# Margins on the steps of chains, an event for the rebuild of x, and later modulation sums in a two-layer diffusion trunk

## The chip, the cores and the metric

The kernel runs on 1 core of one Trainium2 chip. The metric is the device time of one execution in microseconds (us), as the median over repeated runs. The core has the matrix engine TensorE (PE in the rows, its weight loads PEld), VectorE (DVE), ScalarE (ACT), GpSimd (POOL), and SyncE (SP), which starts the DMA transfers here. Each engine works through its own instructions in the order of the program and waits for the others by semaphores.

## The reference

One inference step of a trunk with two layers for 640 tokens (128 context tokens and 512 latent ones) of width 1024. Each layer has a mixer and an MLP:

```python
def _block(x, mod, mixer, g, b, w1, w2):
    sh1, sc1, gt1, sh2, sc2, gt2 = jnp.split(mod, 6, axis=-1)
    mix, aux = mixer(x * (1 + sc1) + sh1)
    x = _layer_norm(ALPHA * x + gt1 * mix, g[0], b[0])
    hf = x * (1 + sc2) + sh2
    ff = jnp.square(jax.nn.relu(hf @ w1)) @ w2
    x = _layer_norm(ALPHA * x + gt2 * ff, g[1], b[1])
    return x, aux
...
mod_ctx = jnp.einsum('d,lde->le', jax.nn.silu(c_ctx), w_mod) + b_mod
mod_lat = jnp.einsum('bd,lde->lbe', jax.nn.silu(c), w_mod) + b_mod[:, None, :]
```

The mixer of layer 0 (even) is retention beside differential attention, that of layer 1 (odd) windowed attention beside gated linear attention (GLA). Both have one input projection and one output projection. The MLP goes from 1024 to 4096 and back. The modulation vector `mod` of a layer has 6 x 1024 values for each of two conditions (context, latent), and costs a pass over a 1024 x 6144 weight.

## The kernel before, in words

The 640 tokens are 5 tiles of 128. Every large matmul is made of three products of fp32r halves: a weight is split into `whi` (a cast on ACT) and `wlo` (a subtraction on DVE), an activation likewise (`hh`/`hl`, `cath`/`catl`, `ghi`/`glo`), and PE sums hi x hi, hi x lo and lo x hi. A step of 24 matmuls (8 chunks of the contraction by 3 products) is the unit in which the program is written.

The program is laid out by a planner in Python, the class `Order`. It keeps a model clock `now` and a queue of modelled operations for each engine. `product` moves `now` on with each matmul, so the written order of PE is the program order. For the other engines the order is that in which the model starts the operations, and it is pinned with dependencies (`follow`). On the chip each engine then keeps to that order whatever the true times are; the model has no say in when something runs.

Small work is written as generators, the *chains*: `spawn` starts one, a chain yields between its steps, and `ready` decides when its next step may be written. A bare `yield` means that all operations issued by the step before must have ended in the model; a number means a delay in model time; a callable means an event. `gemm` writes one large matmul step: first every chain that is ready, then `background()` (splits and loads of weights, and a step of the modulation every few us of model time), then the matmuls. So a chain's transposes and small matmuls stand in PE's order between the large steps, and the large steps that stand between a chain's last vector operation and the matmul that reads it are its *cover*.

Names that the prediction uses:

- **Modulation.** A chunk of 512 columns is made of 8 pieces of `w_mod`, loaded by DMA into `wmod` (3 buffers, `MRAW`). POOL multiplies a piece by the conditioning column and adds it into its accumulator `moda` (a TENSOR_SCALAR and a TENSOR_TENSOR), DVE does the other condition into a `moda` of its own, whose first piece ACT writes. `ModChunk.finish` then has PE sum over the partitions (`modps`, ones x `moda`), and DVE adds the bias (`brow`). In layer 0 this goes on through the mixer and the MLP, for the chunks that come later.
- **norm** (L859): the layer norm of a token tile after the output projection (key "m") and after the MLP (key "h"). It normalises `x` on POOL, transposes it (`lnT`), applies modulation into `hh`/`hl` for the matmuls that come next, and starts `update()`: x = x * g + b, in place, four TENSOR_TENSOR of 128x512 on POOL for a tile, `x<-x,lnrow` in the rows, 20 for the five tiles. The sum that reads this x comes only at the end of the next mixer or MLP.
- **Even mixer.** Per head: `qkT` transposes, `sd` scores, softmax `p`, `wT` transposes, `odp` products, normed `od`, `catT` transposes into `cath`/`catl`. `U` are the state products of retention.
- **Odd mixer.** At its end: `po` (GLA's output in PSUM), copies to `o` on ACT, head norm (`hbn`, `hmv`, `hve`, `rsq`, `nmr` on DVE, then `o<-o,nmr,rsq` on ACT), the gate `o<-o,sg` on POOL, `catT` transposes, `cath` (ACT) and `catl` (DVE), then the output projection `ops`. The output projection is made in two halves of the contraction, env 0 and env 1: 240 matmuls of the first half (5 tiles x 2 column halves x 24) can run before GLA is done; the second half reads `catT` of `o`.
- **MLP.** Eight groups of 512 hidden units, g0 to g7. A group is `ff` (192 matmuls, ~28 us), relu squared (`relu`, `ghi`, `glo`), then `fps` (five token tiles t, 24 matmuls each) and `y` sums.

Of the kernel before, what the change touches and what calls it, by code (L numbers as in the profile page):

```python
# [35 lines left out]
DEC0, DEC = 0.0, 2.0  # L36
MOD_SPACE = (4.0, 3.6)
LO_POOL = 0
UPD = (40.0, 30.0)
DRS = False  # L40
WD = 3
WS = 2
MRAW = 3
NSMALL = 4


C_ID = 0
# [80 lines left out]
class Order:  # L128
# [181 lines left out]
        self.chains.append(c)  # L310

    def ready(self, c):
        if c[2] > self.now or not all(self.over(x) for x in c[1]):
            return False
        if c[3] == "s":
            return any(self.vacant(x) for x in self.rings.get("s", [None]))
        return c[3] is None or c[3]()
# [87 lines left out]
def trunk_kernel(ctx: ExitStack, tc: tile.TileContext, io: dict, layers: int = 2, stop: str = ""):  # L405
# [21 lines left out]
    def slot(s):  # L427
        t = gpool.tile([P, SLOT], F32, tag="g", name=nm(s))
        order.ring_of[t.tensor.name] = "g"
        return t  # L430
# [118 lines left out]
    class ModChunk:  # L549
# [36 lines left out]
        def finish(self):  # L586

            l, a = self.l, self.c % 2
            kind = self.c // 2
            if a == 0:  # L590
                mods[l, kind] = dram.tile([2, 2, 512], F32, name=nm("mrow"))
            ps = acc("modps")
            b = self.b
            for j in range(4):
                mm(ps[32 * j:32 * j + 32, :256], ones[:, 0:32], self.A[j % 2][:, 256 * (j // 2):256 * (j // 2) + 256],
                   start=True, stop=True)
            dve.tensor_tensor(b[:, :256], ps[:, :256], b[:, :256], op=ALU.add)
            for r in range(2):
                load(mods[l, kind][r, a, :].rearrange("(e n) -> e n", e=2), b[32 * r:32 * r + 65:64, :256])
            if kind not in (2, 5):  # L600
                if a == 0:
                    cols[l, kind] = const.tile([P, 8, 2], F32, name=nm("mcol"))
                for r in range(2):
                    load(cols[l, kind][:, 4 * a:4 * a + 4, r], mods[l, kind][r, a, :].rearrange("(b p) -> p b", p=P))
            done.add(("mod", l, self.c))
            yield 0.0

    done = set()
# [247 lines left out]
            pool.tensor_tensor(y, y, rows[1 if t == 0 else 0][a][:, :512], op=ALU.mult)  # L856
            stt(x, x, ALPHA, y, op0=ALU.mult, op1=ALU.add)

    def norm(t, rows, ft, A, B, final, key, xd=None):  # L859

        cuts = [(0, 0, 512), (1, 0, 512)] if t < NT - 1 else [(0, 0, 256), (0, 256, 512), (1, 0, 256), (1, 256, 512)]
        st = sm("bn", [P, 4, 6])[:, :len(cuts), :]
        mv = sm("mv", [P, 2])
        for i, (a, c0, c1) in enumerate(cuts):
            dve.bn_stats(st[:, i, :], X[t][a][:, c0:c1])
        dve.bn_aggr(mv, st)
        if DRS:
            ve = sm("ve", [P, 1])
            dve.tensor_scalar(ve, mv[:, 1:2], EPS, None, op0=ALU.add)
            r = rsqrt(ve, [P, 1])  # L870
        else:
            ve = sm("ve", [P, 1])
            sq = sm("sq", [P, 1])
            act.activation(sq, mv[:, 1:2], AF.Sqrt, bias=eps_t)
            dve.tensor_scalar(ve, mv[:, 1:2], EPS, None, op0=ALU.add)
            r = sm("r", [P, 1])
            q = sm("q", [P, 1])
            dve.reciprocal(r, sq)
            vec_tt(q, r, r, op=ALU.mult)
            stt(q, q, -0.5, ve, op0=ALU.mult, op1=ALU.mult)  # L880
            stt(r, q, 1.5, r, op0=ALU.add, op1=ALU.mult)
        nmr = sm("nmr", [P, 1])
        stt(nmr, mv[:, 0:1], -1.0, r, op0=ALU.mult, op1=ALU.mult)
        if not final:
            xn = X[t]
            for a in range(2):
                pool.tensor_scalar(xn[a][:, :512], xn[a][:, :512], r, nmr, op0=ALU.mult, op1=ALU.add)
        time = order.step[:]
        if final:

            cut = (1024, 1024, 1024, 512, 256)[t]
            for a, c0, c1 in ((0, 0, 256), (0, 256, 512), (1, 0, 512)) if t == NT - 1 else ((0, 0, 512), (1, 0, 512)):
                c, far = slice(c0, c1), 512 * a + c1 <= cut
                x, g, b = X[t][a][:, c], rows[0][a][:, c], rows[1][a][:, c]
                if far:
                    act.activation(x, x, AF.Identity, scale=r, bias=nmr)
                    pool.tensor_tensor(x, x, g, op=ALU.mult)
                    pool.tensor_tensor(x, x, b, op=ALU.add)
                else:
                    stt(x, x, mv[:, 0:1], g, op0=ALU.subtract, op1=ALU.mult)  # L900
                    stt(x, x, r, b, op0=ALU.mult, op1=ALU.add)
                load(io["y"][t * P:(t + 1) * P, 512 * a + c.start:512 * a + c.stop], x)
            return
        def update():
            for a in range(2):
                x = xn[a][:, :512]
                pool.tensor_tensor(x, x, rows[0][a][:, :512], op=ALU.mult)
                pool.tensor_tensor(x, x, rows[1][a][:, :512], op=ALU.add)
                yield 3.0
            if xd is not None:  # L910
                for a in range(2):
                    load(xd[a], xn[a][:, :512])
            done.add(("x", *key))
        yield time
        yield "s"
        tp = pss("lnT")
        for k in range(KT):
            transpose(tp[:, tcol(k)], xn[k // 4][:, tcol(k % 4)])
        r_ = 1 if t == 0 else 0
        for a in range(2):  # L920
            h = slot("h32")
            for b in range(4):
                k = 4 * a + b
                act.activation(h[:, tcol(b)], tp[:, tcol(k)], AF.Identity,
                                     scale=A[:, k, r_:r_ + 1], bias=B[:, k, r_:r_ + 1])
            h4 = h[:, :512].rearrange("p (b c) -> p b c", b=4)
            hi = ft.h[a][:, :, tcol(t)]
            act.copy(hi, h4)
            (pool if a < LO_POOL and t < NT - 1 else dve).tensor_tensor(ft.l[a][:, :, tcol(t)], h4, hi.bitcast(F32), op=ALU.subtract)
        order.spawn(update(), UPD[xd is not None])  # L930
        yield
        done.add(key)

# [3 lines left out]
    ft = FT("h0")  # L937
# [542 lines left out]
    def odd_mixer(ft, cat, out_half):  # L1480
# [208 lines left out]
        def sq(m):  # L1689
            st = W[m]  # L1690
            st["q"] = [slot("sqT"), slot("sqT")]

            def post(t, ps):
                qq = slot("qq")
                if t == 0:
                    act.copy(qq[:, :256], ps[:, :256])
                else:
                    a = rope(ps[:, :256], t, 4)
                    vec_tt(qq[:, :256], a[:, :256], a[:, 256:512], op=ALU.add)

                def turn():
                    tp = acc("sqT")
                    for b in range(2):
                        transpose(tp[:, tcol(b)], qq[:, tcol(b)])
                    for b in range(2):
                        act.copy(st["q"][b][:, tcol(t)], tp[:, tcol(b)])
                later(turn)
            project((1, f"SQ{m}"), ft, post)
# [114 lines left out]
        gqk(0)  # L1823
        value_project((1, "GV0"), ft, G[0].vs)
        order.spawn(gla_chain(0))
        sq(0)
        later(lambda: swa(0), 3.5)
        gqk(1)
# [35 lines left out]
    def layer(l, ft, xd):  # L1864
# [26 lines left out]
        for t in range(NT):  # L1891
            for a in range(2):
                order.gemm(lambda: out_projection(l, cat, env, 1, t, a), cond)
            order.spawn(norm(t, ln, ft, A, B, False, ("m", l, t)))
        del cat, env


        rows = None
        for g in range(8):
            last = g == 7  # L1900
            parts = [(slot("ghi")[:, :TOK].bitcast(F32R), slot("glo")[:, :TOK].bitcast(F32R)) for _ in range(4)]
            if g == 0:
                mod_hold[0] = False
# [42 lines left out]
            if not last:  # L1946
                for nh in range(2):
                    for t in range(NT):
                        order.gemm(lambda: mlp_block(t, nh), lambda: g < 6 or ("x", "m", l, t) in done)
            else:  # L1950
                ln = ln_rows(l, 1)
                ft_n = A = B = None
                if not last_layer:
                    need_mods(l + 1, (0, 1))
                    mod_hold[0] = True
                    A, B = norm_cols(l, 1)
                    ft_n = FT("h")
                xd = [[dram.tile([P, 512], F32, name=nm("xd")) for _ in range(2)] for _ in range(NT)]
                for t in range(NT):
                    for nh in range(2):  # L1960
                        order.gemm(lambda: mlp_block(t, nh))
                    order.spawn(norm(t, ln, ft_n, A, B, last_layer, ("h", l, t), xd[t]))
        if last_layer:
            order.drain(lambda: not order.chains)
            return None, None
# [114 lines left out]
```

## Time and profile before

| what | value |
|---|---|
| median of 3 runs | 1718.78 us (1714.31 to 1721.03) |
| the profiled execution | 1719.93 us, span of its trace 1718.1 us |
| busy share of the span | PE 93%, DVE 64%, ACT 38%, POOL 42% |
| mean granted clock of PE | 0.965 of full speed |

The trace is one execution. Its span is 1.8 us shorter than its own time, and its time lies 1.15 us above the median. The share of an engine is its busy time over the span; PE's chain of work decides the end, so the rows to look for are those where PE stands idle or runs at a lower clock.

### The profile page before, as it was taken

What the parts mean: (1) busy time and instruction counts of PE and PEld (TensorE: products, weight loads), DVE (VectorE), ACT (ScalarE), POOL (GpSimd) and SP (SyncE); (2) the same over time, 40 slices, a digit from 0 to 9 for tenths busy, and PEclk for the clock granted to TensorE, in tenths of its full rate; (3) what the DMA queues carried; (4) which work ended last, traced back from release to release, by engine and by line L of the source; (5) the groups of instructions that cost most, each with busy time, mean ns of one, the idle gap of its engine ahead of it and who ended that gap; (6) DMA issues with size and microseconds to landing.
All of it is one profiled execution on the core that took longest, in us unless ns stands there. A gap on an engine that the chain in (4) does not pass through costs nothing.

```text
span 1718.1 us, 27804 instructions
## 1 busy us (share of the span) xinstructions
PE 1592.2 (93%) x10869; PEld 1437.5 (84%) x10869; DVE 1096.0 (64%) x1953; ACT 649.8 (38%) x1338; POOL 727.4 (42%) x625
## 2 busy tenths in 40 slices
PE   7888989989888999999899999979989999999995
PEld 4887888889777998898688988869979889988994
DVE  2787875588656666776757678777862444434458
ACT  2564554344431322232126645554443223222221
POOL 1786666671595556555705535431170000000115
PEclk9998999999899999999999999989989999999998
DMA  9432333452245545445232311113212222223221
GB/s 336 155 95 88 108 94 105 126 171 72 69 126 147 142 139 162 137 143 166 86 93 81 114 51 46 30 53 114 75 63 85 74 74 74 74 74 99 74 74 61
DMA packets 89522, 178.22 MB, mean 104 GB/s; under 512 B 23360, under 2 KB 30512, under 8 KB 89392
## 3 DMA queue, kind: packets, MB, share of 16 engines
q1 hardware_dynamic: 89392, 176.46, 32.8%
q8 instruction: 85, 1.39, 0.3%
q14 instruction: 45, 0.37, 0.1%
HBM read 169.92 MB, written 6.50 MB: 103 GB/s over the span
## 4 chain that ended last, share of the span: by engine, by line
PE 70%; DVE 14%; POOL 7%; ACT 4%; issue 3%; DMA 2%; SPq 0%; POOLq 0%; ACTq 0%; DVEq 0%
PE ff L467 24%; PE fps L467 22%; PE proj L467 8%; PE ops L467 4%; POOL moda L377 3%; PE fproj L467 2%; DMA wmod<-in_w_mod 2%; POOL wmod L377 2%; DVE wlo L377 2%; PE early L467 1%; PE po L467 1%; DVE hl L377 1%; POOL x L377 1%; DVE x L377 1%; PE gl L467 1%
## 5 line engine op out<-in xcount | busy, mean ns | idle before, releaser
L467 PE MATMUL ff<-hl,whi 128*128 128x320 f32 (+2 forms) x1024 | 319.8, 312 | 8.8 <-DVE hl L377 8.8
L467 PE MATMUL ff<-hh,whi 128*128 128x320 f32 (+2 forms) x1024 | 321.0, 313 | 4.5 <-ACT hh L377 4.5
L467 PE MATMUL ff<-hh,wlo 128*128 128x320 f32 (+2 forms) x1024 | 319.7, 312 | 3.2 <-DVE wlo L377 3.2
L377 ACT CAST whi<-wraw 128x1024 fp32r<-128x1024 f32 (+1 forms) x187 | 193.8, 1043 | 284.2 <-PE fps L467 220.2
L377 DVE TENSOR_TENSOR wlo<-wraw,whi 128x1024 fp32r<-128x1024 f32 (+1 forms) x187 | 250.3, 1343 | 63.6 <-ACT whi L377 63.3
L467 PE MATMUL fps<-wlo,ghi 128*128 128x512 f32 (+1 forms) x648 | 254.2, 392 | 2.0 <-DVE wlo L377 2.0
L467 PE MATMUL fps<-whi,ghi 128*128 128x512 f32 (+1 forms) x648 | 255.0, 394 | 0.0
L467 PE MATMUL fps<-whi,glo 128*128 128x512 f32 (+1 forms) x648 | 253.9, 392 | 0.0
L377 POOL TENSOR_SCALAR wmod<-wmod,cs 128x512 f32<-128x512 f32 x140 | 141.2, 1009 | 155.3 <-DVE moda L377 132.9
L377 POOL TENSOR_TENSOR moda<-moda,wmod 128x512 f32<-128x512 f32 x140 | 201.6, 1440 | 9.1
L467 PEld LDWEIGHTS ff<-hl,whi 128*128 128x128 f32 x1024 | 195.4, 191 | 10.0 <-DVE hl L377 9.4
L467 PEld LDWEIGHTS ff<-hh,whi 128*128 128x128 f32 x1024 | 195.4, 191 | 8.9 <-ACT hh L377 5.0
L467 PEld LDWEIGHTS ff<-hh,wlo 128*128 128x128 f32 x1024 | 195.3, 191 | 4.0 <-DVE wlo L377 4.0
L377 DVE TENSOR_TENSOR relu<-relu 128x320 f32<-128x320 f32 (+3 forms) x100 | 66.6, 666 | 198.0 <-ACT ghi L377 197.5
L377 POOL TENSOR_TENSOR y<-y,gate 128x512 f32<-128x512 f32 x20 | 33.1, 1659 | 357.2 <-DVE y L377 355.7
L377 ACT ACTIVATE relu<-ff 128x320 f32<-128x320 f32 (+3 forms) x100 | 51.3, 513 | 319.1 <-PE ff L467 319.1
L377 DVE TENSOR_TENSOR y<-fps,y 128x512 f32<-128x512 f32 x120 | 82.5, 689 | 118.1 <-PE fps L467 118.1
L467 PEld LDWEIGHTS fps<-wlo,ghi 128*128 128x128 f32 x648 | 122.0, 188 | 30.2 <-DVE wlo L377 3.3
L467 PEld LDWEIGHTS fps<-whi,ghi 128*128 128x128 f32 x648 | 122.1, 188 | 29.3 <-issue 2.0
L467 PEld LDWEIGHTS fps<-whi,glo 128*128 128x128 f32 x648 | 122.0, 188 | 28.2
L377 POOL TENSOR_TENSOR x<-x,lnrow 128x512 f32<-128x512 f32 (+1 forms) x76 | 113.3, 1510 | 47.0 <-ACT x L377 45.5
L377 POOL TENSOR_TENSOR moda<-moda,modp 128x512 f32<-128x512 f32 x56 | 82.0, 1465 | 88.7 <-ACT modp L377 88.4
(285 smaller groups left out, 3553.9 us busy)
## 6 DMA issues: line engine op xcount, KB each, us to landing
wraw<-in_w SPq DMA_DIRECT2D x128, 512.0 KB
wmod<-in_w_mod SPq DMA_DIRECT2D x192, 256.0 KB
wraw<-in_w_even SPq DMA_DIRECT2D x24, 512.0 KB
wraw<-in_w_out SPq DMA_DIRECT2D x16, 512.0 KB
wraw<-in_w_odd SPq DMA_DIRECT2D x16, 512.0 KB
gate<-mrow SPq DMA_DIRECT2D x16, 256.0 KB
xT<-in_xT SPq DMA_DIRECT2D x8, 320.0 KB
brow<-in_b_mod SPq DMA_DIRECT2D x40, 64.0 KB
```

The costliest lines, as they stand in the source:

```text
L377: i = f(*a, **k)
L467: nc.tensor.matmul(o, a, b, **kw)
```

## The change: what is written when

Three rules of the planner change. A chain's step is written only when the operations of its step before ended at least 1.5 us of model time ago (`MARGIN`). The `modps` of a chunk are written 10 us of model time later. And `update()` waits for an event in place of a delay of 40 or 30 us: after the output projection for the start of MLP group 1, after the MLP for the start of `sq(0)` in the odd mixer.

```diff
-UPD = (40.0, 30.0)
...
+MARGIN = 1.5
...
     def ready(self, c):
-        if c[2] > self.now or not all(self.over(x) for x in c[1]):
+        if c[2] > self.now or not all(x.end is not None and x.end + MARGIN <= self.now for x in c[1]):
             return False
...
             kind = self.c // 2
+            yield 10.0
...
-    def norm(t, rows, ft, A, B, final, key, xd=None):
+    def norm(t, rows, ft, A, B, final, key, xd=None, when=None):
...
         def update():
+            yield when
             for a in range(2):
                 x = xn[a][:, :512]
                 pool.tensor_tensor(x, x, rows[0][a][:, :512], op=ALU.mult)
...
-        order.spawn(update(), UPD[xd is not None])
+        order.spawn(update())
...
         order.spawn(gla_chain(0))
+        done.add(("SQ", 0))
         sq(0)
...
-            order.spawn(norm(t, ln, ft, A, B, False, ("m", l, t)))
+            order.spawn(norm(t, ln, ft, A, B, False, ("m", l, t), when=lambda: ("g", l, 1) in done))
...
             last = g == 7
+            if g > 0:
+                done.add(("g", l, g))
...
-                    order.spawn(norm(t, ln, ft_n, A, B, last_layer, ("h", l, t), xd[t]))
+                    order.spawn(norm(t, ln, ft_n, A, B, last_layer, ("h", l, t), xd[t], lambda: ("SQ", 0) in done))
```

Three places of the order that results. The first is PE in group 1 of layer 0's MLP, at the sum of the chunk whose accumulators end in 5688 and 5689 (before), 5670 and 5671 (after). Before:

```order
2805 L467 MATMUL modps_6000<-moda_5688,ones 32x256
2806 L467 MATMUL modps_6000<-moda_5689,ones 32x256
2807 L467 MATMUL modps_6000<-moda_5688,ones 32x256
2808 L467 MATMUL modps_6000<-moda_5689,ones 32x256
2809 L467 MATMUL ff_6018<-hh_4674,whi_5659 128x320
```

After:

```order
2924 L467 MATMUL fps_6196<-whi_6052,glo_5709 128x512
2925 L467 MATMUL modps_6210<-moda_5670,ones 32x256
2926 L467 MATMUL modps_6210<-moda_5671,ones 32x256
2927 L467 MATMUL modps_6210<-moda_5670,ones 32x256
2928 L467 MATMUL modps_6210<-moda_5671,ones 32x256
2929 L467 MATMUL fps_6228<-whi_5959,ghi_5702 128x512
```

The four rows of the sum moved 120 rows back, from inside `ff` to behind the fourth token tile of `fps`; the sums that stand in the later groups moved by 60 each.

The second place is the same group on the engines beside PE. POOL before interleaves `x<-x,lnrow` with the modulation (six more `x` rows stand just ahead of these):

```order
228 L377 TENSOR_TENSOR x_4499<-x_4499,lnrow_4662 128x512
229 L377 TENSOR_TENSOR moda_5475<-moda_5475,wmod_4548 128x512
230 L377 TENSOR_TENSOR x_4499<-x_4499,lnrow_4666 128x512
231 L377 TENSOR_SCALAR wmod_5472<-wmod_5472,cs 128x512
232 L377 TENSOR_TENSOR x_4356<-x_4356,lnrow_4660 128x512
233 L377 TENSOR_TENSOR moda_5475<-moda_5475,wmod_5472 128x512
234 L377 TENSOR_SCALAR wmod_5478<-wmod_5478,cs 128x512
```

POOL after, where the 20 rows of `x` run from 236 to 258 with three rows of modulation among them:

```order
234 L377 TENSOR_TENSOR moda_5469<-moda_5469,wmod_5580 128x512
235 L377 TENSOR_SCALAR moda_5671<-wmod_5601,cs 128x512
236 L377 TENSOR_TENSOR x_4127<-x_4127,lnrow_4647 128x512
237 L377 TENSOR_TENSOR x_4284<-x_4284,lnrow_4647 128x512
238 L377 TENSOR_TENSOR x_4127<-x_4127,lnrow_4651 128x512
239 L377 TENSOR_TENSOR x_4284<-x_4284,lnrow_4651 128x512
240 L377 TENSOR_TENSOR x_4318<-x_4318,lnrow_4647 128x512
```

ACT after, in the same group; `moda_6004<-wmod_5921` is the first piece of the next chunk, and the two rows behind it finish the last hidden tile of the group:

```order
446 L377 ACTIVATE relu_1109_5995<-ff_5970 128x320
447 L377 ACTIVATE ghi_5708<-relu_1109_5995 128x320
448 L377 CAST whi_6052<-wraw_5846 128x1024
449 L377 CAST whi_6075<-wraw_5963 128x1024
450 L377 ACTIVATE moda_6004<-wmod_5921,cs 128x512
451 L377 ACTIVATE relu_1115_6033<-ff_6008 128x320
452 L377 ACTIVATE ghi_5708<-relu_1115_6033 128x320
```

The rows of `x` moved behind the whole of one chunk (5469) and ahead of nearly all of the next (5671). On ACT the start of the chunk after that stands ahead of the last `relu` of the group, as it did before; the `wmod` piece that it reads is loaded into a buffer that POOL frees at its row 265.

The third place is PE at the end of the odd mixer. After, the last rows of `po` are followed at once by the transposes that need them (`o_13119` and `o_13120` are the normed and gated `po`), and these by the second half of the output projection:

```order
6529 L467 MATMUL po_13124<-Sb_12739,gqb_12743 128x128
6530 L467 MATMUL po_13125<-Sb_12739,gqb_12743 128x128
6531 L477 MATMUL catT_13215<-cst,o_13119 128x128 x4
6532 L477 MATMUL catT_13220<-cst,o_13119 128x128
6533 L477 MATMUL catT_13228<-cst,o_13120 128x128 x4
6534 L477 MATMUL catT_13233<-cst,o_13120 128x128
6535 L467 MATMUL ops_13241<-whi_12594,cath_13222 128x256
```

Before, the last `po` is row 6253, then come scores and transposes of the windowed attention and first-half `ops`, the two groups of transposes stand at rows 6357 and 6389, and first-half `ops` go on behind them:

```order
6357 L477 MATMUL catT_12956<-cst,o_12686 128x128 x4
6358 L477 MATMUL catT_12961<-cst,o_12686 128x128
...
6364 L467 MATMUL spo_12969<-pT_12913,sv_9494 64x256
6365 L467 MATMUL ops_12982<-whi_11918,cath_12430 128x256
...
6389 L477 MATMUL catT_13010<-cst,o_12687 128x128 x4
6390 L477 MATMUL catT_13015<-cst,o_12687 128x128
6391 L467 MATMUL ops_13033<-whi_11918,cath_12430 128x256
```

All 240 first-half `ops` moved ahead of `po`, and nothing of PE's stands any more between `po` and its transposes. In the rest of both mixers the same steps stand in the same sequence per head, with some more large matmuls between a chain's steps.

## Rows read from the trace of the kernel before

**Rows 1.** The page: span, PE's share, the chain that ended last, by engine.

```profile
span 1718.1 us, 27804 instructions
...
PE 70%; DVE 14%; POOL 7%; ACT 4%; issue 3%; DMA 2%; SPq 0%; POOLq 0%; ACTq 0%; DVEq 0%
```

The stretches of group 2 are the even mixer, part of layer 0's MLP (the `fps` of group 0 and group 1), and the odd mixer. A row gives start and end, length, the busy us and instructions of PE, PEld, DVE, ACT and POOL, PE's granted clock, and the DMA share and rate.

**Rows 2.** Stretches: even mixer, MLP 459–560, odd mixer.

```profile
72.30:376.20 303.90, 269.24 (x2103) 253.41 (x2101) 223.82 (x518) 156.28 (x379) 204.98 (x167) 0.95 0.36 107
...
459.20:559.80 100.60, 90.65 (x450) 77.26 (x449) 63.93 (x59) 29.20 (x42) 77.97 (x59) 0.95 0.47 139
957.40:1186.60 229.20, 214.03 (x2222) 190.70 (x2221) 175.63 (x427) 122.03 (x316) 93.45 (x112) 0.96 0.19 59
```

**Rows 3.** PE's waits in 459–559 and 844–856: total us, times, longest.

```profile
PE modps L467 <- POOL moda L377: 8.5, 2, 4.6
PE modps L467 <- DVE moda L377: 1.4, 1, 1.4
...
PE modps L467 <- POOL moda L377: 4.3, 1, 4.3
PE modps L467 <- DVE moda L377: 2.1, 1, 2.1
```

**Rows 4.** Stretches right behind those waits (columns as in group 2).

```profile
499.80:503.40 3.60, 3.60 (x18) 3.23 (x13) 0.49 (x2) 0.00 (x0) 3.60 (x5) 0.53 0.82 272
523.80:530.70 6.90, 5.34 (x22) 4.53 (x23) 2.36 (x5) 0.00 (x0) 4.06 (x5) 0.51 0.55 147
848.10:854.90 6.80, 3.60 (x12) 2.31 (x13) 5.61 (x7) 0.00 (x0) 5.53 (x4) 0.50 0.22 77
```

**Rows 5.** POOL, layer 0's MLP: timeline; then all `x` rows of 429–504 (ns min/median/max).

```profile
461.45 0.94 POOL L377 TENSOR_SCALAR wmod<-wmod,cs 128x512 f32<-128x512 f32 x1 [20.33 <-DVE moda L377]
...
499.46 0.69 POOL L377 TENSOR_SCALAR moda<-wmod,cs 128x512 f32<-128x512 f32 x1
...
L377 POOL TENSOR_TENSOR x<-x,lnrow x20: 1281/1444/2280, 429.9 to 502.0; 128x512 f32<-128x512 f32 x20
```

**Rows 6.** POOL's `x` alone in 461–502: busy us (count).

```profile
461.40:502.00 40.60, 20.69 (x13) 0.97 0.44 131
```

**Rows 7.** PE, the chain, DVE and ACT in groups 1 and 7.

```profile
487.13 0.31 PE L467 MATMUL ff<-hh,whi 128*128 128x320 f32 x1
...
856.54 28.18 PE ff L467 x192
...
500.17 3.71 DMA wmod<-in_w_mod
...
533.21 0.49 DVE L377 TENSOR_TENSOR relu<-relu 128x320 f32<-128x320 f32 x1 [4.71 <-ACT ghi L377]
...
532.64 0.47 ACT L377 ACTIVATE ghi<-relu 128x320 fp32r<-128x320 f32 x1
```

**Rows 8.** The end of the odd mixer on PE, POOL, DVE; timeline.

```profile
1166.23 0.39 PE L467 MATMUL po<-Sb,gqb 64*128 64x128 f32 x4
...
1179.15 1.81 POOL L377 TENSOR_TENSOR o<-o,sg 128x640 f32<-128x640 f32 x1 [0.17 <-ACT o L377]
...
1181.10 0.71 PE L477 MATMUL catT<-cst,o 128*128 128x128 f32 x5
...
1182.56 0.67 DVE L377 TENSOR_TENSOR catl<-catT,cath 128x512 fp32r<-128x512 f32 x1
```

**Rows 9.** PE's waits in the even mixer, 72–376 (columns as in group 3).

```profile
PE wT L477 <- DVE p L377: 7.0, 5, 3.5
PE sd L467 <- DVE qkh L377: 4.8, 3, 2.1
PE catT L477 <- ACT od L377: 4.0, 2, 2.1
PE odp L467 <- DVE wTs L377: 3.8, 4, 1.2
```

**Rows 10.** PE's waits in the odd mixer, 957–1187.

```profile
PE proj L467 <- DVE sg L377: 5.7, 1, 5.7
```

## The prediction

> **What bounds the kernel now.** I read the page first: PE is the longest part of the chain that ended last, 70% of it [rows 1]. So time can come only from PE's gaps and from its clock. The windows by stage show where these lie: in the even mixer PE is busy 269.24 of 303.9 us at a clock of 0.95, in the odd mixer 214.03 of 229.2 at 0.96, and in the stretch 459–560 of layer 0's MLP 90.65 of 100.6 at 0.95 [rows 2]. The reader should see that DVE is busy 224 of 304 us in the even mixer, 74%, and 176 of 229 in the odd one, 77%: far from idle where PE waits for it. The waits by name come next. In the MLP PE waits for `moda` alone: 8.5 + 1.4 us in group 1, and 4.3 + 2.1 at its later end [rows 3]. Behind such a wait the clock stands at about half: 0.53, 0.51 and 0.50, over 3.60, 5.34 and 3.60 us of busy PE [rows 4]. In the mixers the waits are many and short, most of them for a vector operation of a chain [rows 9, 10].
>
> I sum against the profiled execution, 1719.9 us, and take off 1.1 us to come to the median.
>
> **1. Later modulation sums.** The three places where PE waited for `moda` now come 60 to 120 matmuls later, some 10 us or more, and the longest wait was 4.6 us. All 8.5 + 1.4 + 4.3 + 2.1 = 16.3 us go. With them goes the half clock: work of 3.60, 5.34 and 3.60 us at half speed would take half of that, so 6.2 us come back. Term: **-22.5**. The cover is the `ff` and `fps` steps that now stand ahead. It fails only if POOL becomes later by more than 10 us, which is the next point.
>
> **2. The rebuild of x in one block.** The 20 TENSOR_TENSOR are the same work as before. Their price is known: 13 of them took 20.69 us [rows 6], 1.59 each; all 20 ranged from 1.28 to 2.28, with a median of 1.44 [rows 5]. What is new is that they stand together, with three rows of modulation inside (some 3.4 us), ahead of the `wmod` pieces that come next. Each piece needs a buffer that POOL frees.
>
> When does the block start? In the trace POOL took up the modulation at 461.45 and came to the next chunk's first row at 499.46 [rows 5]. Of these 38.0 us, 20.7 were `x`. Without them the chunk ends at 478.8 if every load keeps up; I allow 6 us for loads, and take 485 (bounds 479 and 490). Then 20 x 1.59 + 3.4 brings the block to 520.2, and one more add of 1.6 frees a buffer at 521.8.
>
> Now the queue behind it. The next piece is loaded (0.3 to issue, 3.71 [rows 7]), until 525.8. POOL itself works on two pieces that lay ready, about 5.1 us, until 526.9, then a multiply and an add on the fresh piece, 2.5, to 529.4. That frees the buffer of the piece that ACT's `moda` row reads: another 4.0, 533.4. Behind that row on ACT stand the last `relu` and `ghi` of group 1: `moda` 0.7, two of about 0.47, and on DVE two of 0.49 [rows 7], to 536.0.
>
> PE reaches the `fps` that reads this hidden tile earlier. Group 1 starts at 487.13, its 192 `ff` take 28.18 [rows 7], and two token tiles of `fps` and a little more take 6.2: 521.5. So PE waits about 14.5 us at a place where it did not wait before, and 2.5 us more go to the lower clock, as behind the other waits. Term: **+17**, bounds 0 and +23. The later groups have no `x` in POOL's way, so I price nothing there. In layer 1 the same event costs nothing, since POOL has no modulation left to do then, and the block of the odd mixer stands on a POOL that is busy 93 of 229 us [rows 2].
>
> A rule of the Trainium skill bears on the price. The page "GPSIMD Engine Reference", section 8 (Key points), says that GpSimd shares its SBUF interfaces with VectorE and contends with VectorE instructions that have two SBUF inputs. By it an `x` row costs its lower price of 1.28 whenever DVE is not in such an instruction; this trace shows the spread from 1.28 to 2.28 for one shape, which agrees with the rule without proving it. If the whole block ran at 1.28 it would end 6.2 us sooner and the forecast would be 1702. I keep 1.59, because DVE has the same work in that stretch as before.
>
> **3. The end of the odd mixer.** All first-half `ops` now stand ahead of `po`. In the trace the last `po` ended at 1166.62, POOL's second gate of `o` at 1180.96, and the transposes started at 1181.10 without a gap, because spare `ops` had filled the 14.3 us [rows 8]. That fill is gone. DVE then also had work of the windowed attention between the norm's rows, some 2 us, that is now done earlier, so the chain takes 12.3. From the first transpose to the end of `catl` took 2.13 us [rows 8], and the first `ops` reads exactly that. The gap is 14.4 us, and 2.6 us for the clock behind it, as behind the longest wait of the modulation. Term: **+17**, bounds +14 and +20. Nothing hides it: what could have, the 17 us of first-half `ops` that stood behind the transposes, has run before. The work of PE itself is unchanged, so earlier gaps must shrink for this to be paid back; that is term 4.
>
> **4. The margin in the mixers.** A chain step is written 1.5 us of model time later, so that much more large matmul work stands in front of it. The upper bound of the gain: each wait shrinks by 1.5. The five for `p` (7.0 in all, longest 3.5) lose at least 5.0; `odp` (four, longest 1.2) all 3.8; `catT` (two, 4.0) 3.0; `sd` loses 1.5, since in two of its three places it still follows its transposes directly [rows 9]. That is 13.3 of 19.6. The other gaps of the even mixer are 34.7 - 19.6 = 15.1, spread over many places, some of which keep their cover as it was; a third of them gives 5. Bound 18. I take two thirds, 12, since DVE is at 74% and every delayed step also delays the vector work behind it. The clock: 5% of 269 us, 13.5 us, go with 34.7 us of gaps, 0.39 for 1; 12 us of gaps give 4. Term: **-16**, bounds -30 and +5. In the odd mixer the gaps are 15.2 us, the longest 5.7 for `sg` [rows 10]; by the same share (18 of 34.7) the bound is 8, and I take 4.5, a little under two thirds as DVE is fuller, and 1.5 for the clock. Term: **-6**, bounds -17 and +5. Between mixer and MLP a norm's transposes move both earlier and later; I take nothing, within 5 either way.
>
> **The sum.** -22.5 + 17 + 17 - 16 - 6 = -10.5. 1719.9 - 10.5 - 1.1 = **1708**. What one measurement of this kernel can tell from no change is 0.5%, so below 1710.2 is faster and above 1727.4 slower.
>
> **The rivals.**
>
> *The block does not catch PE.* For it: POOL's start at 485 is an estimate, and if loads keep up and the rows cost 1.28 to 1.44 the buffers come free 9 to 12 us sooner. Against it: seven dependent steps of load, POOL, ACT and DVE follow the block, some 15 us, which no cover takes. 1708 - 17 = 1691.
>
> *The margin buys nothing in the mixers (slower).* Place: the steps between `sd`, `p`, `wT` and `odp`, and their like in the odd mixer. A later matmul makes the next vector step later by as much, and on a DVE at 74 to 77% the queue is what PE waits for; the waits move along the chain and their sum stays. Price: the 22 us of term 4. For it: the busy shares [rows 2]. Against it: the waits are mostly under 2 us [rows 9], the size of the margin. 1708 + 22 = 1730. It decides from where the mixers give back less than 3 us (1727.4).
>
> *It does nothing on balance.* Half of term 4 comes, and the end of the odd mixer and the block are paid: 1708 + 11 = 1719. For it: terms 2 and 3 are gaps that the change makes itself, of the size of those that it takes away.
>
> **Chances.** The forecast 0.45, no wait behind the block 0.20, nothing on balance 0.18, the mixers give nothing 0.17. The forecast's own range, from the bounds of its terms, is 1697 to 1716. Of its 0.45 about 0.32 lies below 1710.2. Faster: 0.32 + 0.20 = 0.52. Slower: 0.17, and 0.04 from the upper edge of the third rival, 0.21. The same: 0.27. The range takes in the first rival's middle and the slower one's: 1688 to 1730.
>
> **What would show it.** In the trace after: no PE wait for `moda` in layer 0's MLP (term 1); one wait of `fps` in group 1 for DVE `glo`, 10 to 15 us, with ACT's `moda` row just ahead of it and POOL in a block of `x` from about 485 to 520 (term 2); one wait of `catT` for POOL `o` at the end of the odd mixer, 11 to 13 us, followed by one for `catl` (term 3); gaps of the even mixer near 23 us and of the odd one near 25 with the new one inside (term 4). I am wrong if the block's wait is missing, if `po` still finds work behind it, or if the even mixer's gaps stay near 35.

## The result, and the profile after

The changed kernel takes 1729.76 us (median of 4 runs, 1728.16 to 1731.14) against 1717.98 us for the kernel before (median of 4 runs, one more than in the table above); the ratio is 1.0073, with a 95% interval of 1.0056 to 1.0090. It is 0.7% slower, where I forecast 10 us faster.

The page of the kernel after, in the two lines that answer to [rows 1]:

```profile
span 1727.1 us, 27818 instructions
...
PE 69%; DVE 16%; POOL 5%; ACT 4%; issue 3%; DMA 2%; SPq 0%; POOLq 0%; ACTq 0%; DVEq 0%
```

The span is 9.0 us longer. To see where, I cut both traces at the same eight points of PE's program. The stretches of the kernel after are: even mixer with its output projection, `ff` of MLP group 0, the rest of groups 0 and 1, groups 2 to 6, group 7 and the boundary to layer 1 up to the first gates, odd mixer with its output projection, `ff` of group 0 of layer 1, the rest. Columns as in [rows 2].

```profile
67.70:414.70 347.00, 310.47 (x2449) 294.38 (x2447) 264.14 (x597) 171.35 (x411) 219.91 (x180) 0.95 0.35 107
414.70:449.50 34.80, 31.13 (x210) 30.31 (x209) 20.44 (x41) 22.45 (x50) 3.87 (x5) 1.00 0.18 61
449.50:550.60 101.10, 89.07 (x450) 75.19 (x450) 70.66 (x60) 29.66 (x42) 92.10 (x65) 0.93 0.44 139
550.60:837.30 286.70, 286.70 (x1633) 254.57 (x1632) 196.22 (x226) 77.60 (x108) 178.81 (x141) 1.00 0.47 144
837.30:941.40 104.10, 95.00 (x580) 87.75 (x579) 70.53 (x134) 42.84 (x107) 40.20 (x34) 0.95 0.23 72
941.40:1241.30 299.90, 272.16 (x2662) 247.52 (x2661) 220.39 (x516) 144.01 (x357) 101.49 (x119) 0.94 0.21 67
1241.30:1285.50 44.20, 35.74 (x211) 34.60 (x210) 37.77 (x41) 22.77 (x50) 35.48 (x24) 0.88 0.15 48
1285.50:1727.10 441.60, 420.36 (x2317) 377.72 (x2315) 201.62 (x289) 117.32 (x167) 38.12 (x26) 0.98 0.24 78
```

The same stretches of the kernel before took 348.0, 41.9, 100.5, 296.6, 95.1, 284.6, 42.2 and 439.8 us, and the start 69.4 in place of 67.7. Beside my terms:

| stretch | forecast | measured |
|---|---|---|
| start | 0 | -1.7 |
| even mixer | -16 | -1.0 |
| `ff` of group 0 | 0 | -7.1 |
| groups 0 and 1 (sums, block) | -14.3 + 17 | +0.6 |
| groups 2 to 6 (sums) | -8.2 | -9.9 |
| group 7 and boundary to layer 1 | 0 | +9.0 |
| odd mixer | -6 + 17 | +15.3 |
| `ff` of group 0 of layer 1, rest | 0 | +3.8 |

**Group 1** went as described in step 2. PE's waits in 459–559 of the kernel after were, in place of those of [rows 3]:

```profile
PE fps L467 <- ACT ghi L377: 10.3, 1, 10.3
PE fps L467 <- DVE glo L377: 1.6, 1, 1.6
```

and the timeline shows the chain behind them, POOL first, then ACT and PE:

```profile
473.94 0.69 POOL L377 TENSOR_SCALAR moda<-wmod,cs 128x512 f32<-128x512 f32 x1
474.60 15.21 POOL L377 TENSOR_TENSOR x<-x,lnrow 128x512 f32<-128x512 f32 x9
...
493.52 15.66 POOL L377 TENSOR_TENSOR x<-x,lnrow 128x512 f32<-128x512 f32 x9
...
510.37 1.52 POOL L377 TENSOR_TENSOR x<-x,lnrow 128x512 f32<-128x512 f32 x1
...
524.88 0.72 ACT L377 ACTIVATE moda<-wmod,cs 128x512 f32<-128x512 f32 x1 [17.31 <-DMA wmod<-in_w_mod]
525.51 0.42 ACT L377 ACTIVATE relu<-ff 128x320 f32<-128x320 f32 x1
525.96 0.47 ACT L377 ACTIVATE ghi<-relu 128x320 fp32r<-128x320 f32 x1
...
526.48 0.80 PE L467 MATMUL fps<-whi,ghi 128*128 128x512 f32 x1 [10.29 <-ACT ghi L377]
```

The reader sees the block of 20 rows of `x` from 474.60 to 511.89, ACT idle for 17.31 us for a piece of `wmod` whose buffer POOL freed late (its add ended at 521.66, SyncE issued the load at 521.69), and the `relu` that PE needs queued behind it. The kernel reached group 1 about 9.6 us earlier than before (477.5 against 487.1), so the block began 2.9 us ahead of the group; I had put it 2.1 ahead.

**The end of the odd mixer** shows the gap of step 3, at 9.83 + 0.59 us where I had 14.4:

```profile
1202.54 1.33 PE L477 MATMUL catT<-cst,o 128*128 128x128 f32 x5 [9.83 <-POOL o L377]
1204.47 1.33 PE L477 MATMUL catT<-cst,o 128*128 128x128 f32 x5 [0.59 <-POOL o L377]
```

**The even mixer** kept its gaps: 348.0 - 312.0 = 36.0 us before, 347.0 - 310.5 = 36.5 after. But their names changed. PE's waits there in the kernel after, beside [rows 9]:

```profile
PE sd L467 <- ACT p L377: 7.4, 4, 4.7
PE ops L467 <- DVE tmp L377: 5.5, 2, 4.2
PE sd L467 <- DVE qkh L377: 3.1, 2, 1.8
PE proj L467 <- DVE ropea L377: 2.6, 1, 2.6
...
PE wT L477 <- DVE p L377: 0.9, 1, 0.9
```

The waits that I counted on did go: `wT` for `p` fell from 7.0 to 0.9, those of `odp` and of `catT` for `od` are no longer listed. Others of the same sum took their places. One profile of a mixer holds only to a few us: six kernels whose layer 0 is planned alike up to its MLP (e2, e6, e8, e11, e12, e17 below) took 342.7 to 346.7 us there.

### The profile page after: what moved, and what is told of

Same layout as the page of the kernel before. It is cut to its first block, busy times and chain, and to the rows that moved or that the text cites. A ratio compares the mean times of both kernels' runs of the same rounds, so it can differ in the third digit from the quotient of the medians.

```text
span 1727.1 us, 27818 instructions
## 1 busy us (share of the span) xinstructions
PE 1592.9 (92%) x10869; PEld 1440.7 (83%) x10869; DVE 1110.9 (64%) x1953; ACT 650.4 (38%) x1338; POOL 739.7 (43%) x625
## 4 chain that ended last, share of the span: by engine, by line
PE 69%; DVE 16%; POOL 5%; ACT 4%; issue 3%; DMA 2%; SPq 0%; POOLq 0%; ACTq 0%; DVEq 0%
PE ff L467 24%; PE fps L467 23%; PE proj L467 8%; PE ops L467 4%; DVE wlo L377 2%; PE fproj L467 2%; POOL x L377 2%; PE early L467 2%; POOL moda L377 1%; DVE rsqa L377 1%; DVE mx L377 1%; POOL wmod L377 1%; PE po L467 1%; DMA wmod<-in_w_mod 1%; DVE x L377 1%
## 5 line engine op out<-in xcount | busy, mean ns | idle before, releaser
L377 DVE TENSOR_TENSOR wlo<-wraw,whi 128x1024 fp32r<-128x1024 f32 (+1 forms) x187 | 258.3, 1385 | 59.6 <-ACT whi L377 59.5
L377 ACT CAST whi<-wraw 128x1024 fp32r<-128x1024 f32 (+1 forms) x187 | 193.6, 1044 | 251.0 <-PE fps L467 241.1
L467 PE MATMUL fps<-whi,ghi 128*128 128x512 f32 (+1 forms) x648 | 255.8, 395 | 10.3 <-ACT ghi L377 10.3
L377 POOL TENSOR_SCALAR wmod<-wmod,cs 128x512 f32<-128x512 f32 x140 | 152.0, 1086 | 137.0 <-DVE moda L377 109.4
L377 DVE TENSOR_TENSOR relu<-relu 128x320 f32<-128x320 f32 (+3 forms) x100 | 70.7, 707 | 190.4 <-ACT ghi L377 190.4
L377 POOL TENSOR_TENSOR x<-x,lnrow 128x512 f32<-128x512 f32 (+1 forms) x76 | 117.9, 1583 | 48.3 <-ACT x L377 48.1
```

The costliest lines, as they stand in the source:

```text
L377: i = f(*a, **k)
L467: nc.tensor.matmul(o, a, b, **kw)
```

## The experiments

All times below are medians beside a kernel before that ran on the same chip, at 1716.4 to 1718.5 us; a bracket is the 95% interval of the ratio to it.

### One part at a time

The margin alone, the later sums alone, the events alone, and the change without the margin; each is a piece of the diff shown above.

> Before plus the 1.5 us margin alone; sums and rebuild of x as before. Theory A, the margin is what made the changed kernel slower: its gaps at the layer boundary (about +8), in the odd mixer with the bare transposes at its end (about +15) and the shorter boundary ahead of layer 0's MLP (about -7) all come with it, the even mixer stays, so 1718 + 15 = about 1733. The transposes after po have 24 first-half ops (2.9 us) ahead of them here instead of none, so the wait there should be about 7 in place of 9.8. Theory B, the events did it and the margin helps as forecast: about 1705.

1733.0 us, ratio 1.0091 [1.0075, 1.0108]. Theory A. The odd mixer took 298.8 us (284.6 before), the boundary 102.5 (95.1), the even mixer 348.2. But `ff` of group 0 took 40.8: the 7 us that were won there are not the margin's. In groups 0 to 6 the margin alone won 13.3 us (383.8 against 397.1), since the chain that writes the sums keeps the margin too: PE's waits for `moda` fell from 16.4 to 6.4 us. So the later sums and the margin share part of one gain.

> Before plus the 10 us delay of the modulation sums alone; on PE only these sums move. Theory A: the five waits for moda (16.3 us) and the half clock behind them (6.2) go, nothing takes their place: about 1697. Theory B: POOL is the limit there and the waits come back at the later sums, or as waits for DVE: 1710 to 1718.

1700.3 us, 0.9899 [0.9885, 0.9912]. The later groups gave 9.5 us (287.1), as theory A says. Groups 0 and 1 gave 5.2 us (95.3) of the 14.3 that I had booked: a wait of 6.5 us for `glo` took the place of those for `moda`, since ACT's queue already stood behind a late `wmod`:

```profile
518.47 0.72 ACT L377 ACTIVATE moda<-wmod,cs 128x512 f32<-128x512 f32 x1 [9.80 <-DMA wmod<-in_w_mod]
```

So interleaved `x` rows hold up that load too. In the kernel before, the same ACT row waited 1.55 us for its piece, at 521.99, and PE, late by its waits for `moda`, did not feel it. In e10 below, with 4 rows of `x` in that stretch in place of 14, the row starts at 506.14 without a wait.

> Before plus the events for the rebuild of x alone. Theory A: the block of x on POOL is as in the changed kernel, the sums are not later, so the waits for moda in group 1 grow and the wait for ghi comes on top or inside them: gaps of group 1 from 10 to 15-20 us, about 1724 to 1730. Odd mixer as before within 5. Theory B: the block is paid by the chain of loads only, and sums and ghi wait for the same thing: 1718 to 1722.

1730.1 us, 1.0064 [1.0052, 1.0077]. The total is that of theory A, its place is not: groups 0 and 1 took 104.9 (100.5 before), but the odd mixer 303.2 in place of 284.6. I had priced the event there at nothing.

> The changed kernel without the margin (sums later and events remain). Theory A, the margin is the loss: the wait for ghi in group 1 remains (about 10), the later groups keep their -10, and odd mixer and boundaries are as before: about 1709. Theory B, the events also move the boundary and the odd mixer: 1718 to 1728.

1719.5 us, 1.0008 [0.9997, 1.0019]. Theory B: the odd mixer takes 305.1 without any margin. `ff` of group 0 took 36.8: the gain there is the event's.

### Which event, which layer

Base is the kernel with the later sums alone, 1700.3 us.

```diff
 e5: norm(..., ("m", l, t), when=lambda: ("g", l, 1) in done)     # UPD stays for "h"
 e6: norm(..., ("h", l, t), xd[t], lambda: ("SQ", 0) in done)     # UPD stays for "m"
 e7, e8: x.end + order.margin <= self.now, with order.margin = (1.5, 0.0)[l] and (0.0, 1.5)[l]
```

> Base is the kernel with the later sums alone (1700.3). Added: the event for the rebuild of x in layer 0's and layer 1's MLP alone; the rebuild after the MLP keeps its delay. Theory A: the wait for ghi in group 1 comes back (10 us of wait, group 1 from 67.4 to about 72), the run-up to layer 0's MLP gets 5 shorter since no x stands in POOL's way beside VectorE's hl there, the odd mixer is untouched: about 1700, within 2. Theory B: the block costs its wait and gives nothing back: 1705 to 1712.

1698.3 us, 0.9885 [0.9869, 0.9902]. Theory A: 4.5 us won in `ff` of group 0 (36.8 against 41.3), 5.6 lost behind it (100.9 against 95.3). The gain has a plain cause in the trace: with no `x<-x,lnrow` on POOL, VectorE's `hl` of 128x512 took 0.69 us in the median, 0.84 at most. In the kernel before it took up to 1.75 beside these rows, and PE waited 4.3 us for it:

```profile
429.95 9.54 POOL L377 TENSOR_TENSOR x<-x,lnrow 128x512 f32<-128x512 f32 x6
433.81 1.75 DVE L377 TENSOR_TENSOR hl<-h,hh 128x512 fp32r<-128x512 f32 x1
...
PE ff L467 <- DVE hl L377: 4.3, 1, 4.3
```

> Base is the kernel with the later sums alone (1700.3). Added: the event for the rebuild of x after layer 0's MLP alone. Theory A: this event alone is what costs some 20 us in the odd mixer without the margin, because the block of x on POOL lies beside the first gates of the odd mixer, where VectorE is then slower and PE waits for it: about 1719. Theory B, the loss in the odd mixer comes from both events together: below 1710.

1718.4 us, 1.0009 [0.9998, 1.0020]. Theory A: this event alone costs 18 us, in the odd mixer (302.8 against 284.8). Its timeline at the first gates, POOL, DVE and PE:

```profile
955.58 14.38 POOL L377 TENSOR_TENSOR x<-x,lnrow 128x512 f32<-128x512 f32 x9
...
971.33 2.54 POOL L377 TENSOR_TENSOR Eq<-gA 128x320 f32<-128x320 f32 x2
...
966.51 2.31 DVE L377 TENSOR_TENSOR wlo<-wraw,whi 128x1024 fp32r<-128x1024 f32 x1
...
971.94 1.35 DVE L377 TENSOR_TENSOR Ek<-Ek,gkT 128x640 f32<-128x640 f32 x1
...
985.65 0.82 DVE L377 TENSOR_TENSOR Ek<-Ek,gkT 128x640 f32<-128x640 f32 x1
...
980.52 0.66 PE L477 MATMUL sqT<-cst,qq 128*128 128x128 f32 x2 [5.88 <-DVE ropea L377]
```

The block stands among the gates of GLA, and PE waits 5.88 us where it had not waited. VectorE is slower beside POOL's rows: `wlo` takes 2.31 us beside the `x` rows (1.22 in the median), `Ek` 1.35 beside `Eq<-gA` and 0.82 while POOL is idle. But that is not what PE waits for: e2, without the event, has an `Ek` of 1.35 too, and e12 below shows the same wait, 5.9 us, with the `x` rows cut to 8 columns.

> Base is the kernel with the later sums alone (1700.3). Added: the margin in layer 0 alone (layer 1 plans without it). Theory A: the waits of the even mixer move and do not shrink (within 2 of 0), but the boundary to layer 1 and the MLP change by some us: 1697 to 1706. Theory B, the forecast of the margin: 16 less, 1684.

1706.3 us, 0.9927 [0.9910, 0.9944]. Theory A, at its upper end: 101.3 at the boundary (95.9), and 349.3 in the even mixer (345.7 in the base), a difference that profiles of one order show too.

> Base is the kernel with the later sums alone (1700.3). Added: the margin in layer 1 alone. Theory A: the end of the odd mixer loses its cover (24 first-half ops left of 240 behind po), the wait of catT for POOL o is about 5 to 10, and the other gaps keep their sum: 14 to 18 more, about 1716. Theory B: the loss in the odd mixer comes from what layer 0 hands over (the order of the transposes at the boundary), and the margin within layer 1 saves some us: 1695.

1722.4 us, 1.0035 [1.0023, 1.0046]. Theory A in place, more in size: odd mixer 298.4 (284.8), and 5 us behind it, where `ff` of group 0 of layer 1 takes 45.7 in place of 41.8.

### The end of the odd mixer, the block, and what the event really costs

```diff
 e9, in out_half of layer 1:
+            order.margin = 0.0
 e10, base e5:
-    when=lambda: ("g", l, 1) in done
+    when=lambda t=t: ("g", l, t + 1) in done
 e11: the planner takes 0.01 us for an x row of update(); e12: it takes 1.226, the row works on [:, :8]
```

> The changed kernel, but in layer 1 the margin ends when the first half of the output projection begins. PE then has 72 first-half ops (8.6 us) between po and its transposes, where the changed kernel has none. Theory A, the loss at the end of the odd mixer is the missing cover: the wait of catT for POOL o falls from 9.8 to under 4 and the half clock behind it goes, some 9 to 12 less than the changed kernel, about 1719. Theory B, the time is lost in the steps before (each chain step later by its margin): less than 4 gained, 1726 or more.

1730.0 us, 1.0068 [1.0056, 1.0080]: nothing gained. The 8.6 us of cover took the wait of `catT` from 9.83 to 6.55 only, and a wait of 5.72 of `ops` for `pT` opened ahead of it; the odd mixer took 300.7. So the bare transposes are where the loss shows, not what makes it: theory A fell, and theory B's number came.

> Base is the kernel with later sums and the event in the MLP (1698.3). Changed: token tile t is rebuilt when group t + 1 of the MLP begins, so POOL gets four rows of x at a time. Theory A, the wait for ghi in group 1 (10 us) comes from the block: it goes, group 1 takes 65 to 67.4 in place of 73.0, and the shorter run-up stays: about 1692. Theory B, the load chain of wmod is late anyway: group 1 stays near 73, 1698.

1686.3 us, 0.9813 [0.9799, 0.9826]. Theory A, and more: groups 0 and 1 have no gap left.

```profile
451.80:537.40 85.60, 85.60 (x450) 73.44 (x449) 61.27 (x59) 29.46 (x42) 66.06 (x50) 1.00 0.53 164
```

Against 101.1 in the kernel after, the block cost 15.5 us there, close to the 17 of step 2. Against the interleaved rows of e2 (95.3) it cost 5.6 (e5): these rows cost 9.7 themselves.

> Later sums and the event after the MLP (1718.4), but the planner counts a row of x as 0.01 us. PE's order at the end of the odd mixer is that of the kernel without the event, while POOL really does all 20 rows among the gates of the odd mixer. Theory A, what costs 18 us is the order that the planner makes when it believes the block to hold up the gates: near 1700 to 1704. Theory B, it is POOL's real work there, beside a slowed VectorE: near 1718.

1709.8 us, 0.9947 [0.9935, 0.9960]; odd mixer 291.3.

> The reverse: the order of the kernel with later sums and the event after the MLP (1718.4), the planner counts each row of x in full, but the rows work on 8 of 512 columns only (x after layer 0's MLP is left mostly unscaled; the work is left out). Theory A, the order is the cost: near 1716. Theory B, POOL's real block is the cost: near 1700.

1717.1 us, 0.9998 [0.9987, 1.0009]; odd mixer 303.4. Both theories hold in part, and the parts do not add up: the block's real work costs 6.5 us (291.3 against 284.8) under the old order; the order that the planner makes for it costs 18.6 (303.4) with hardly any real work behind it, since this kernel leaves most of the rebuild out; both together cost 18.0.

### The serial chain

GLA's two halves are one chain: seven levels, each waiting for the one before, then keys, states and outputs, and the second half starts when the first is free. What can be run beside its end is the first half of the output projection, 240 `ops`, 28.8 us at 2.88 a step of 24. In the kernel before, all of it stands behind the last `po`, 144 `ops`, 17 us, even behind the transposes. The traces, cut at the start of the last `po`:

| odd mixer | before | e8 | after | e6 |
|---|---|---|---|---|
| last `po` behind the first gates, us | 214.8 | 246.1 | 251.0 | 244.5 |
| matmuls ahead of it | 2087 | 2329 | 2387 | 2171 |
| first-half `ops` among them | 0 | 216 | 240 | 72 |
| PE idle ahead of it, us | 15.1 | 17.6 | 14.7 | 26.0 |
| PE idle behind it, us | 1.2 | 8.4 | 13.0 | 1.3 |

There are two losses, not one. With the margin (e8, after) the chain's end stands 242 to 300 matmuls later in PE's order, nearly all first-half `ops` are spent ahead of it, and PE idles behind it. With the event alone (e6) it stands 84 matmuls later, first-half `ops` are left, and PE idles ahead of it, at a clock of 0.92 in place of 0.95. The chain that ends too late explains the first; why the order around the block makes the second is not shown.

```diff
 e13 (the changed kernel); e17 (base e8) does the same with a flag, exempt=True:
-order.spawn(gla_chain(0)) ... order.spawn(second())
+order.spawn(gla_chain(0), margin=0.0) ... order.spawn(second(), margin=0.0)
```

> The changed kernel, but the two GLA chains keep no margin; every other chain does. Theory A, the loss in the odd mixer is the margin on the steps of that serial chain, which ends the mixer: the last po comes some 30 us earlier in the order, first-half ops stand behind it again, and the odd mixer takes 283 to 288 in place of 299.8: about 1715. Theory B, it is the margin on all chains there: above 1724.

1734.4 us, 1.0100 [1.0083, 1.0117]. By its numbers theory B. But it doesn't separate the two costs: the margin on GLA had also moved the gates behind the block of `x`, and without it the block stands among them as in e6 (PE's wait for `ropea` is 6.0). It does show that a late end of the chain is not what the event costs: the last `po` comes 224.0 us behind the first gates, 27 earlier than in the changed kernel, `catT` no longer waits for `o`, and the odd mixer still takes 302.2; PE idles 23.3 us ahead of that `po`.

> The kernel with later sums and the margin in layer 1 (1722.4), without the margin on the two GLA chains, and without the event after the MLP. Theory A, the margin's loss in the odd mixer is the longer GLA chain: the odd mixer, 298.4 there, comes back to 285 to 288, about 1709 with the 5 us that stay lost behind it. Theory B, the margin on the other chains costs it: odd mixer above 294, 1717 or more.

1708.7 us, 0.9948 [0.9936, 0.9961]. Theory A: without the event, taking the margin from the GLA chain alone brings the odd mixer from 298.4 to 286.4. The windows of e8 and then e17 there:

```profile
933.00:1231.40 298.40, 272.34 (x2662) 246.57 (x2661) 219.21 (x516) 144.66 (x357) 103.08 (x123) 0.96 0.19 62
```

```profile
932.00:1218.40 286.40, 264.94 (x2662) 241.18 (x2661) 219.62 (x516) 144.30 (x357) 101.92 (x123) 0.97 0.20 65
```

PE's idle time falls by 4.6 us and its busy time, for the same instructions, by 7.4, at a clock of 0.97 in place of 0.96. Of the busy time some 4 us can be chance: it was 264.0 in e5 and 268.3 in e2 with one order of PE there.

### The margin where it was meant to help

Base is e10, 1686.3 us; the margin ends, or begins, at the output projection of layer 0.

> Base is the kernel with later sums and the rebuild spread over the MLP's groups (1686.3). Added: the margin of 1.5 in the even mixer only, off from its output projection on. Theory A, waits move and keep their sum: even mixer within 3 of the base's 348.6, total 1684 to 1690. Theory B, the forecast: 12 to 16 less there, 1672.

1688.1 us, 0.9834 [0.9814, 0.9854]. Theory A.

> As the run before with a margin of 3.0. Theory A: the same sum again, or some us worse as the chains get longer: 1684 to 1695. Theory B, the gain grows with the margin: below 1672.

1677.7 us, 0.9770 [0.9749, 0.9791]. 8.6 less, between the two theories; the fastest kernel of this study.

> As the run with a margin of 3.0 in the even mixer alone (1677.7), with 4.5. Theory A, the gain of 3.0 is one lucky order among several: within the spread seen at 0 and 1.5, 1680 to 1690. Theory B, more margin is more cover: 1670 or less.

1684.4 us, 0.9807 [0.9790, 0.9824]. The gain does not grow: theory A. The even mixer at margins of 1.5, 3.0 and 4.5:

```profile
68.30:415.00 346.70, 312.35 (x2449) 298.41 (x2447) 261.47 (x591) 172.43 (x411) 220.35 (x180) 0.94 0.36 107
```

```profile
68.50:408.20 339.70, 307.06 (x2449) 293.25 (x2447) 256.13 (x592) 172.01 (x411) 225.94 (x180) 0.95 0.36 109
```

```profile
68.20:417.10 348.90, 312.43 (x2449) 298.10 (x2447) 248.27 (x589) 171.86 (x411) 219.65 (x180) 0.94 0.36 106
```

Without a margin the runs whose layer 0 is planned as in e2 took from 342.7 (e17) to 348.7 (e10). Gaps are 37.6 us in e10 and 34.4, 32.6 and 36.5 here. Only 3.0 lies outside that spread; why its order is better stays open.

> The same base with the margin of 1.5 in layer 0 from the output projection on, none in the mixers. Theory A, the loss at the boundary to layer 1 comes from the margin on the norm's steps there: the stretch from the last fps to the first gates of layer 1 takes 72 to 75 in place of 66.3, 1691 to 1695. Theory B, it came from elsewhere: 1686.

1691.2 us, 0.9847 [0.9832, 0.9861]. Theory A: the boundary takes 103.9 in place of 95.2. PE's waits there:

```profile
PE proj L468 <- DVE ve L378: 3.8, 1, 3.8
PE skT L478 <- DVE kk L378: 3.1, 3, 1.5
```

The same two waits stand in the kernel after. Of the 8.7 us, 4.0 are idle time and 4.7 the same work at a clock of 0.95 in place of 1.00. `ve` belongs to a token tile's norm, `kk` to the keys of the windowed attention: chains whose steps the margin moves. That nothing spare stands beside them is my reading, not tested.

## Why the prediction was wrong

**Step 1 was right** in the later groups (-9.9 for -8.2). In group 1 the sums alone (e2) gave 5.2 us, not 14.3, since the load chain was late already.

**Step 2 was right** in mechanism, by the chain of steps that I had written down: PE's wait came, 10.3 + 1.6 us for 14.5, and against rows in groups of four (e10) the block cost 15.5 us for 17. But beside the order before it cost 4.4 (e3) to 5.6 us (e5), since the interleaved rows already held up the same load. So step 1 was some 9 us too good there and step 2 some 12 too bad; that their sum came right (+0.6 for +2.7) is luck. I missed what the move gave back: no `x` beside VectorE in `ff` of group 0, -7.1 us (4.5 to 6 in e5 and e10). The rule of the Trainium skill that I had weighed (GPSIMD Engine Reference, section 8, the shared interfaces) acts there on VectorE as well: `hl` up to 1.75 us beside `x`, 0.69 without; this trace agrees with it. I had applied it to the price of POOL's rows alone.

**Step 3 had the right place** and nearly the right sum: the gap was 10.4 us and not 14.4, and PE's work took 3.8 us longer in the odd mixer where I had 2.6. The cover is gone because the margin puts the end of the chain later, past nearly all first-half `ops`; e17 takes the margin off that chain alone, and the odd mixer comes back to 286.4. Cover that is put back at that place alone (e9) gains nothing: another wait of 5.7 us opens ahead of it.

**Step 4 failed, and with it the sign.** "Each wait shrinks by 1.5" was true of the waits that I listed, which fell from 19.6 to 4.0 us; the sum of all gaps did not shrink, 36.0 to 36.5 in the even mixer where I had -12 and the clock besides. In the odd one PE idled 14.7 us ahead of the last `po`, 15.1 before, where I had -4.5. That is the slower rival, "the margin buys nothing in the mixers", which gave 1730 and had 0.17. Its price shows as 15.0 us in the even mixer (-1.0 for -16) and inside the +15.3 for +11 of the odd one. Its reason, that PE waits for VectorE's queue, no run shows. The boundaries, which I took at nothing within 5, made +5.7 in sum: -7.1, +9.0 (of it 8.7 by the margin, e16) and, behind the odd mixer, +3.8. The other stretches came out 5.5 us better than their terms, so that the rival's 1730 fits to a microsecond is in part luck.

**In step 2 one sentence was wrong beside that**: that the block in the odd mixer costs nothing, as POOL has room. With the event but no margin it costs 18 us (e6), most of it by the order that the planner makes (e12); a share of 93 of 229 us busy does not show that. In the changed kernel this cost does not appear: the block ends at 945.05, ahead of the gates at 958.93, and PE idles no more ahead of the last `po` than before. With both the odd mixer loses 15.3, not 18 + 14.

What stays open: which resource keeps the sum of the even mixer's gaps near 36 us at margins of 0, 1.5 and 4.5, and why the order around the block costs 18 us where no margin moves the gates.

## What to carry to other kernels

A delay that is added to each step of a serial chain adds up along it (31 us at the end of GLA's chain, e8); count a chain's steps times the delay against the work that can run meanwhile before adding it. That it buys cover elsewhere was not shown here: 1.5 and 4.5 bought nothing in the even mixer, and why 3.0 gave 8.6 us is open. A busy share does not show what a block of work costs on a side engine: ask which queue stands behind the block, who waits for that, and which neighbour slows down; four rows at a time (e10) left no gap where twenty in a row cost 15.5 us. When a listed wait is removed, look in the same stretch for the next latest operand before booking the gain.

## What was not expected of the hardware

VectorE's operations with two inputs slowed by 1.6 to 2.5 times beside POOL's TENSOR_TENSOR rows: `hl` of 128x512 up to 1.75 us against 0.69 and `wlo` of 128x1024 2.31 against 1.22 beside `x`, `Ek` of 128x640 1.35 against 0.82 beside `Eq<-gA`. POOL's own rows went from 1.28 up to 2.28 us before. The Trainium skill (GPSIMD Engine Reference, section 8) names this contention; the sizes are this case's.
